# A one-layer trunk on one core: first products of the later MLP blocks run ahead, the second half's norm placed between them, stores issued from GpSimd

## The chip, the core and the metric

The kernel is one program on one NeuronCore of a Trainium2 chip. Its engines are TensorE (PE, with a separate row for weight loads, PEld), VectorE (DVE), ScalarE (ACT), GpSimd (POOL) and SyncE (SP, which here only issues DMA transfers). The metric is the device time of one execution in microseconds (us); lower is better.

## The reference

One layer over 1024 tokens with 1024 features, all in float32. What matters here is the order of the norms and the size of the MLP:

```python
z = rms_norm(h) @ w_in                 # input projection
...                                    # convolution, attention, short convolution, pooling
h = h + rms_norm(mix @ w_out)          # mix: the four mixers side by side
hn = rms_norm(h)
ff = jnp.square(relu(hn @ w_up)) @ w_down       # 1024 -> 4096 -> 1024
h = h + rms_norm(ff)
gate = sigmoid(rms_norm(h) @ w_gate)
h = h + rms_norm((p @ w_proj) * gate)
```

Each rms_norm needs a sum over all 1024 features of a token, so no column of `hn` is known before every block of `mix @ w_out` for that token is done.

## The kernel before

Everything is held transposed: features on the 128 partitions, tokens along a row. The 1024 tokens are two halves of 512 (hf 0 and hf 1). A float32 operand is split in two pieces, hi and lo, one by an ACT cast (L127) and one by a DVE subtraction (L128), and each product of two blocks is three matmuls (hi·hi, hi·lo, lo·hi) of 128x512.

The stages follow one another: input projection and mixers, `out_proj(0)`, `out_proj(1)` (8 blocks of 24 matmuls each, for one half of the tokens), the MLP, and the gate with the output.

The MLP is cut by features in four blocks, c = 0 to 3, each an up group and a down group. A group is one Strassen-Winograd step with seven products, named by p and run in the order 1, 2, 6, 5, 7, 4, 3 (`ORD`). A product is 48 matmuls: four output blocks (mp) of twelve. For an up group the operand on the right is `hn` in quarters: p=1 and p=2 use quarters of the first half of the tokens alone; p=6 and those after it use sums in which both halves stand. So p=1 and p=2 need only `mix_norm(0)`, and the others `mix_norm(1)` too. The right operands of p=1, 2, 6, ... are written to `t_d` in DRAM once, and read back by the later blocks (`Stored`).

`mix_norm(hf)` is the two norms between `out_proj` and the MLP: a sum of squares over blocks, the column sums on PE (L190), a short chain of small DVE operations (L193 to L202), a broadcast on PE (L204) that ACT copies to SBUF (L206), then per block a multiply by it (L806), the residual from `xT` added (L807), the store to `h_d`, a square on ACT (L215) and a sum on DVE (L216); then again L190 to L206, and the scaling L816. The `xT` blocks come through two buffers (`R2`).

Each engine works through its instructions in the written order, apart from small moves of a scheduler; generators in `bg` are advanced by `pump` between products. SP issues every load and nearly every store, in one queue: a store in it waits for the operation that makes its data, and all that stands behind waits too. Before the change SP holds 52 stores of this part (8 `m_d`, 16 `h_d`, 28 `t_d`).

In the old order PE does: `out_proj(1)` with `mix_norm(0)` between its blocks, L190 and L204 of `mix_norm(1)`, p=1 of block 0, p=1 of block 1 (`g1a`, kept in the two `Q` tiles by `Early`), p=2 of block 0, then p=6 of block 0 and the rest. MLP weights come by 1 MB loads (4 for each group) into the six `raw` buffers of 8 KB a partition, which are opened only when the mixers' buffers are closed, after `out_proj(1)`.

What comes ahead of a product is prepared during the product before it: `prep_left` (sums of weight quarters on DVE, 128x2048 each), `prep_right` (right operand), `prep_piece` (hi and lo of one half of the weights).

Of the kernel before, what the change touches and what calls it, by code (L numbers as in the profile page):

```python
# [48 lines left out]
def trunk_layer(ctx, tc, xT, xt, pT, vec, w_in, w_vf, w_pw, w_pool, w_out, w_up, w_down,  # L49
# [6 lines left out]
    psp = ctx.enter_context(tc.tile_pool(name="psp", bufs=1, space=bass.MemoryType.PSUM))  # L56

    BUFS = {"X": 8, "Q": 2, "XS": 6, "F": 8, "U": 2, "W": 4, "TM": 4, "R2": 2, "TC": 5, "TY": 2, "B": 2,
            "P": 2, "V": 4, "PT": 2, "R": 2, "raw": 6, "WG": 10, "G": 1, "GR": 2}
    pools = {}  # L60

    def open_pools(stack, *tags):
        for t in tags:
            pools[t] = stack.enter_context(tc.tile_pool(name=f"p{t}", bufs=1, reuse_waits="tile"))

    open_pools(ctx, "X", "Q", "XS", "F", "U", "W", "TM", "R2", "TC", "TY", "B")
    mixer = ExitStack()
    open_pools(mixer, "P", "V", "PT", "R")
    cnt = [0]

    def uid(s):
# [51 lines left out]
    def store(dst, src, q=nc.sync):  # L123
        q.dma_start(out=dst, in_=src)
# [628 lines left out]
    sq1 = [None, None]  # L753
    mg = [None] * KT

    def out_proj(hf, npump):
        sq1[hf] = tmp("TY")
        for ft in range(KT):
            wh, wl = ws.get(f"o{ft}")
            ps = bank()  # L760
            for i, k in enumerate(YORD):
                spread(i, npump, 10 if hf == 0 else 0)
                mm3(ps, wh[:, k], wl[:, k], y[k][hf][:, 0], y[k][hf][:, 1], i == 0, i == KT - 1)
            with tc.high_priority():
                acc_sq(ps, sq1[hf], ft == 0)
            if hf == 0:
                m = tmp()
            else:
                if ft % 2 == 0:
                    mg2 = slot("F", [P, 2, HALF])  # L770
                m = mg2[:, ft % 2]
                mg[ft] = m
            with tc.high_priority():
                nc.scalar.activation(m, ps, AF.Copy, scale=vcol("g_mix_post", ft))
            if hf == 0:
                store(m_d[ft], m)
# [5 lines left out]
    def split_t(i, k, src):  # L782
        t = slot("X", [P, 2, HALF], F32R)
        split(src, t[:, 0], t[:, 1])
        if i is not None:
            store(t_d[i, k], t.bitcast(F32))
        return t

    t1st = {}
# [1 line left out]
    def mix_norm(hf):  # L791
        bc = rstd_from_sq([sq1[hf]], HALF, 1.0 / D)
        yield
        sq2 = tmp("TY")
        ms = []
        for ft in range(KT):
            if hf == 0:
                if ft % 2 == 0:
                    m2 = slot("U" if ft < 4 else "F", [P, 2, HALF])
                m = m2[:, ft % 2]  # L800
                load(m, m_d[ft])
            else:
                m = mg[ft]
            raw = aux()
            load(raw, xT[ft][:, hs(hf)])
            nc.vector.tensor_mul(m, m, bc)  # L806
            nc.vector.tensor_add(m, m, raw)  # L807
            store(h_d[ft][:, hs(hf)], m)
            acc_sq(m, sq2, ft == 0, "TC")
            ms.append(m)  # L810
            yield
        bc2 = rstd_from_sq([sq2], HALF, 1.0 / D)
        yield
        hq[0, hf], hq[1, hf] = ms[0:4], ms[4:8]
# [6 lines left out]
    load_y(0)
    out_proj(0, 16)
    pump(1000)
    pumpc(1000)
    load_y(1)
    bg.append(mix_norm(0))
    out_proj(1, 3)
    pump(100)
    mixer.close()
    top = ExitStack()  # L830
    open_pools(top, "raw")


    ff = [None] * KT
    sqf = [None, None]

    class Group:

# [2 lines left out]
            self.kind, self.c, self.a = kind, c, {}  # L841

        def load(self, i, j):
            r = self.a[i, j] = slot("raw", [P, 2048])
            if self.kind == "up":
                f = 8 * self.c + 4 * i
                load(r.rearrange("p (m k n) -> p m k n", m=4, k=4),
                     w_up[f:f + 4, :, 4 * j:4 * j + 4].rearrange("m p k n -> p m k n"))
            else:
                load(r.rearrange("p (b k n) -> p b k n", b=2, k=4),  # L850
                     w_down[2 * self.c + j, 2 * i:2 * i + 2].rearrange("b p k n -> p b k n"))

        def combine(self, p):

            a = self.a
            if p == 1:
                return a[0, 0]
            if p == 2:
                return a[0, 1]
            if p == 6:  # L860
                nc.vector.tensor_sub(a[0, 0], a[0, 0], a[1, 0])
                s2 = a["s2"] = slot("raw", [P, 2048])
                nc.vector.tensor_sub(s2, a[1, 1], a[0, 0])
                nc.vector.tensor_add(a[1, 0], a[1, 0], a[1, 1])
# [76 lines left out]
    class Up:  # L941
# [29 lines left out]
        def out(self, p, mp, ps):  # L971
# [23 lines left out]
            else:  # L995
                add(r[0, 1], ps, r[0, 1])
                self.act(r[0, 1])

    class Early:


        def __init__(self):
            q = [slot("Q", [P, 2, HALF]) for _ in range(2)]
            self.p1 = [q[i // 2][:, i % 2] for i in range(4)]

        def start(self, p):
            pass

        def out(self, p, mp, ps):
            nc.scalar.copy(self.p1[mp], ps)  # L1010

    class Down:

# [69 lines left out]
    def product(n, pump_n=0):  # L1083
        p, g, right, outs, banks = seq[n]
        if n + 1 < len(seq):
            prep_left(n + 1)
            prep_right(n + 1)
            prep_piece(n + 1, 0)
        outs.start(p)
        t, s, _ = prepared.pop(n)  # L1090
        key = g, banks or CHAIN[p]
        new = key not in held
        held.setdefault(key, [])
        for mp in range(4):
            if new:
                held[key].append(bank(SETS[key[1]][mp]))
            ps = held[key][mp]
            for k in range(4):
                lh, ll = g.cols(s[mp // 2], mp, k)
                first = new and k == 0  # L1100
                mm(ps, lhsT=lh, rhs=t[k][:, 0], start=first, stop=False, skip_group_check=True)  # L1101
                mm(ps, lhsT=lh, rhs=t[k][:, 1], start=False, stop=False, skip_group_check=True)  # L1102
                end[0] = mm(ps, lhsT=ll, rhs=t[k][:, 0], start=False, stop=(k == 3), skip_group_check=True)  # L1103
            outs.out(p, mp, ps)
            pump(pump_n)
            if mp == 1 and n + 1 < len(seq):
                prep_piece(n + 1, 1)
                loads_after(n + 1)
# [92 lines left out]
    g1a = Group("up", 1)
    ups[0].load(0, 0)
    g1a.load(0, 0)
    ups[0].load(0, 1)
    ups[0].load(1, 0)
    ups[0].load(1, 1)
    early = Early()
    given = Given(t1st)
    first = Up(0)
    seq.append((1, ups[0], given, first, None))  # L1210
    seq.append((1, g1a, given, early, "C"))
    seq.append((2, ups[0], given, first, None))
    right0 = Right(hq, True)
    add_group(ups[0], right0, first, ORD[2:])
    add_group(downs[0], Right(first.r, False), Down(0, False), ORD)
    for c in range(1, 4):
        u = Up(c, early.p1 if c == 1 else None)
        add_group(ups[c], Stored(), u, ORD[1:] if c == 1 else ORD)
        last = c == 3
        add_group(downs[c], Right(u.r, False), Down(c, last), (1, 2, 6, 7, 4, 5, 3) if last else ORD)  # L1220
    prep_left(0)
    prep_right(0)
    for h in range(2):
        prep_piece(0, h)
    for _ in mix_norm(1):
        pass
    for n in range(len(seq)):
        if n == len(seq) - 2:
            bg.append(ff_norm(0))
        product(n, 2 if n >= len(seq) - 2 else 0)  # L1230
# [95 lines left out]
```

## Time and profile before

| | |
|---|---|
| three runs | 1189.30, 1193.99, 1195.81 us; median 1193.99 |
| the profiled execution | 1192.21 us, its span 1190.5 us |
| PE busy | 1142.7 us, 96% of the span |
| DVE busy | 882.8 us, 74% |
| ACT busy | 603.1 us, 51% |
| POOL busy | 15.3 us, 1% |
| mean granted TensorE clock | 0.982 |

The span is what the profile sees of the 1192.21 us; 1.7 us lie outside it. An engine's busy time says how full it is over all stages, and PE's busy time also counts stretches in which its clock was granted at half: such a stretch is busy and yet lasts twice as long. The granted clock is therefore read beside busy time; 1.00 is 2.4 GHz, 0.50 is 1.2 GHz.

### The profile page before, as it was taken

The numbers are of one execution on the slowest core, as the hardware profiler recorded it, in microseconds if no ns is written. First come the engines' busy times: TensorE is split into PE (matmuls) and PEld (weight loads), VectorE is DVE, ScalarE is ACT, GpSimd is POOL, SyncE is SP. The second block draws the span as 40 slices with busy tenths as digits, with TensorE's granted clock in tenths as the row PEclk, the third lists the DMA queues.
The fourth block names the chain that finished last, engine by engine and source line by source line (L and its number), as shares of the span: only waits on it lengthen the run. The fifth ranks groups of instructions, "written<-read, shape, count | busy, mean of one in ns | idle before, by whom it ended". The sixth has DMA issues, their size and how long they took to land.

```text
span 1190.5 us, 14348 instructions
## 1 busy us (share of the span) xinstructions
PE 1142.7 (96%) x5276; PEld 926.1 (78%) x5276; DVE 882.8 (74%) x1419; ACT 603.1 (51%) x1001; POOL 15.3 (1%) x40
## 2 busy tenths in 40 slices
PE   7999999999999969699999999999999999998997
PEld 5788868778878748588888888888888888886876
DVE  6489679986944788859864599734997439999765
ACT  6511474565654445466533654246542455555664
POOL 2100000000000000000000000000000000000000
PEclk9999999999999979899999999999999999999899
DMA  8311121110445775570337503576034760024243
GB/s 319 127 47 54 62 80 37 45 45 27 131 149 190 247 296 181 197 269 29 107 133 258 210 1 107 177 274 220 1 106 134 273 230 1 1 97 150 80 133 124
DMA packets 58885, 159.16 MB, mean 134 GB/s; under 512 B 5952, under 2 KB 6080, under 8 KB 58816
## 3 DMA queue, kind: packets, MB, share of 16 engines
q1 hardware_dynamic: 57536, 154.06, 37.0%
q0 software_dynamic: 1280, 4.20, 0.9%
q8 instruction: 41, 0.67, 0.2%
q14 instruction: 28, 0.23, 0.1%
HBM read 124.68 MB, written 33.55 MB: 133 GB/s over the span
## 4 chain that ended last, share of the span: by engine, by line
PE 82%; DVE 8%; DMA 4%; ACT 3%; issue 2%; SPq 0%; POOL 0%; DVEq 0%; ACTq 0%; POOLq 0%
PE pm L163 7%; PE pm L164 7%; PE pm L165 7%; PE pm L1103 5%; PE pm L1102 5%; PE pS L1103 5%; PE pS L1102 5%; PE pm L1101 5%; PE pS L1101 5%; PE pT L1103 4%; PE pT L1101 4%; PE pT L1102 4%; PE pV L1102 2%; PE pV L1101 2%; PE pV L1103 2%
## 5 line engine op out<-in xcount | busy, mean ns | idle before, releaser
L127 ACT CAST XS<-raw 128x1024 fp32r<-128x1024 f32 x112 | 117.6, 1052 | 154.0 <-PE pm L1102 44.6
L128 DVE TENSOR_TENSOR XS<-raw,XS 128x1024 fp32r<-128x1024 f32 x112 | 136.5, 1220 | 71.5 <-ACT XS L127 71.0
L1101 PE MATMUL pm<-X,XS 128*128 128x512 f32 x248 | 98.5, 398 | 13.3 <-ACT X L127 8.5
L1103 PE MATMUL pm<-X,XS 128*128 128x512 f32 x248 | 97.8, 394 | 2.1 <-DVE XS L128 2.1
L1102 PE MATMUL pm<-X,XS 128*128 128x512 f32 x248 | 98.1, 396 | 0.9 <-DVE X L128 0.9
L1101 PE MATMUL pS<-X,XS 128*128 128x512 f32 x248 | 96.7, 391 | 0.0
L1102 PE MATMUL pS<-X,XS 128*128 128x512 f32 x248 | 96.5, 389 | 0.0
L1103 PE MATMUL pS<-X,XS 128*128 128x512 f32 x248 | 96.5, 389 | 0.0
L1102 PE MATMUL pT<-X,XS 128*128 128x512 f32 x236 | 92.6, 393 | 0.0
L1103 PE MATMUL pT<-X,XS 128*128 128x512 f32 x236 | 91.9, 389 | 0.0
L1101 PE MATMUL pT<-X,XS 128*128 128x512 f32 x236 | 91.8, 389 | 0.0
L380 DVE SCALAR_TENSOR_TENSOR TC<-U,vecs,TC 128x512 f32<-128x512 f32 (+17 forms) x120 | 86.3, 737 | 2.2 <-ACT TC L376 0.8
L163 PE MATMUL pm<-X,W 128*128 128x512 f32 x192 | 79.2, 413 | 0.0
L164 PE MATMUL pm<-X,W 128*128 128x512 f32 x192 | 77.9, 406 | 0.0
L165 PE MATMUL pm<-X,W 128*128 128x512 f32 x192 | 76.9, 400 | 0.0
L128 DVE TENSOR_TENSOR W<-R,W 128x1024 fp32r<-128x1024 f32 (+1 forms) x34 | 41.6, 1222 | 36.2 <-ACT W L127 35.9
L1101 PEld LDWEIGHTS pm<-X,XS 128*128 128x128 f32 x248 | 47.6, 192 | 25.1 <-ACT X L127 9.0
L127 ACT CAST W<-R 128x1024 fp32r<-128x1024 f32 (+1 forms) x34 | 35.7, 1049 | 50.9 <-PE pm L164 45.5
L1103 PEld LDWEIGHTS pm<-X,XS 128*128 128x128 f32 x248 | 47.4, 191 | 12.7 <-DVE XS L128 2.8
L1102 PEld LDWEIGHTS pm<-X,XS 128*128 128x128 f32 x248 | 47.4, 191 | 11.5 <-DVE X L128 1.6
L1101 PEld LDWEIGHTS pS<-X,XS 128*128 128x128 f32 x248 | 46.9, 189 | 9.8
L1103 PEld LDWEIGHTS pS<-X,XS 128*128 128x128 f32 x248 | 46.5, 187 | 9.7
(528 smaller groups left out, 2763.9 us busy)
## 6 DMA issues: line engine op xcount, KB each, us to landing
X<-t_d SPq DMA_DIRECT2D x80, 512.0 KB, 6.0
raw<-in_w_up_dram SPq DMA_DIRECT2D x17, 1024.0 KB, 5.1
raw<-in_w_down_dram SPq DMA_DIRECT2D x16, 1024.0 KB, 5.1
t_d<-X SPq DMA_DIRECT2D x28, 512.0 KB, 3.5
R<-in_w_in_dram SPq DMA_DIRECT2D x16, 512.0 KB, 3.5
R<-in_w_out_dram SPq DMA_DIRECT2D x16, 512.0 KB, 3.6
F<-in_xt_dram SPq DMA_DIRECT2D x8, 512.0 KB, 7.8
proj_d<-TM POOLq DMA_DIRECT2D x16, 256.0 KB, 4.7
```

The costliest lines, as they stand in the source:

```text
L127: copy(hi, raw)
L128: nc.vector.tensor_sub(lo, raw, hi)
L163: mm(ps, lhsT=lh, rhs=rh, start=first, stop=False)
L164: mm(ps, lhsT=lh, rhs=rl, start=False, stop=False)
L165: end[0] = mm(ps, lhsT=ll, rhs=rh, start=False, stop=last)
L380: nc.vector.scalar_tensor_tensor(acc[j][:, lo:], u[j][:, o + lo - s:o + HALF - s], vcol("w_dw", j * TAPS + TAPS - 1 - s), acc[j][:, lo:], ...
L1101: mm(ps, lhsT=lh, rhs=t[k][:, 0], start=first, stop=False, skip_group_check=True)
L1102: mm(ps, lhsT=lh, rhs=t[k][:, 1], start=False, stop=False, skip_group_check=True)
L1103: end[0] = mm(ps, lhsT=ll, rhs=t[k][:, 0], start=False, stop=(k == 3), skip_group_check=True)
```

## The change

The buffers of 8 KB a partition are shared out anew. The pool `P` (two tiles, used by attention) stays open to the end; `raw` has 4 buffers instead of 6, and a ring (`wslot`) hands out P, P, raw, raw, raw, raw. Gate weights, which had ten `WG` tiles, now have six and four halves of P tiles.

The sequence of products starts with p=1 of blocks 1, 2 and 3 (`pre`), then p=1 and p=2 of block 0. Block 1's result is kept in `Q` as before; those of blocks 2 and 3 go through `TM` to DRAM (`p1_d`) and come back into `Q` ahead of their block's p=2. Blocks 2 and 3 then run six products instead of seven, and their p=6, 5 and 4 add the early result on DVE where ACT copied before: 24 additions of 128x512. The number of products in all is unchanged.

`mix_norm(1)` is pumped, two steps behind each block of the first products. The second broadcast of each norm is put behind PE's latest product (`issue_after`), for hf 0 three steps later. The weights of the first two products are loaded into the P tiles ahead of `out_proj(1)`, and split into pieces from its sixth block on, as written; the scheduler places the first pieces at attention's end. The stores to `m_d`, `h_d`, `t_d` and `p1_d` (60 in all) are issued from GpSimd.

```diff
-            "P": 2, "V": 4, "PT": 2, "R": 2, "raw": 6, "WG": 10, "G": 1, "GR": 2}
+            "P": 2, "V": 4, "PT": 2, "R": 2, "raw": 4, "WG": 6, "G": 1, "GR": 2}
...
-                store(m_d[ft], m)
+                store(m_d[ft], m, nc.gpsimd)
...
-            store(t_d[i, k], t.bitcast(F32))
+            store(t_d[i, k], t.bitcast(F32), nc.gpsimd)
...
-            store(h_d[ft][:, hs(hf)], m)
+            store(h_d[ft][:, hs(hf)], m, nc.gpsimd)
...
-        bc2 = rstd_from_sq([sq2], HALF, 1.0 / D)
+        if hf == 0:
+            for _ in range(3):
+                yield
+        with tc.issue_after(end[0].ins):
+            bc2 = rstd_from_sq([sq2], HALF, 1.0 / D)
...
+    def wslot():
+        ring[0] += 1
+        return slot("P" if (ring[0] - 1) % 6 < 2 else "raw", [P, 2048])
...
         def out(self, p, mp, ps):
-            nc.scalar.copy(self.p1[mp], ps)
+            t = self.p1[mp] if self.keep else tmp()
+            nc.scalar.copy(t, ps)
+            if not self.keep:
+                store(p1_d[self.c, mp], t, nc.gpsimd)
...
+    early = [Early(c, c == 1) for c in range(1, 4)]
+    pre = [Group("up", c) for c in range(1, 4)]
+    for c in range(3):
+        seq.append((1, pre[c], given, early[c], "AC"[c % 2 == 0]))
     seq.append((1, ups[0], given, first, None))
-    seq.append((1, g1a, given, early, "C"))
     seq.append((2, ups[0], given, first, None))
...
-        u = Up(c, early.p1 if c == 1 else None)
-        add_group(ups[c], Stored(), u, ORD[1:] if c == 1 else ORD)
+        blk = Up(c, early[c - 1])
+        add_group(ups[c], Stored(), blk, ORD[1:])
...
+    pre[0].load(0, 0)
+    pre[1].load(0, 0)
     load_y(1)
     bg.append(mix_norm(0))
-    out_proj(1, 3)
+    out_proj(1, 3, first_left)
     pump(100)
+    prep_right(0)
     mixer.close()
...
-    for _ in mix_norm(1):
-        pass
+    bg.append(mix_norm(1))
     for n in range(len(seq)):
...
-        product(n, 2 if n >= len(seq) - 2 else 0)
+        if n == npre - 1:
+            pump(100)
+        product(n, 2 if n < npre - 1 or n >= len(seq) - 2 else 0)
```

The order on PE, where `out_proj(1)` ends. Before, its last matmuls (L163 to L165) are followed by the two PE steps of `mix_norm(1)`'s first norm, and then by the first product (L1101 to L1103):

```order
L164 MATMUL pm_4030<-PT_3614,W_3996 128x512
L165 MATMUL pm_4030<-PT_3614,W_3997 128x512
L190 MATMUL pc_4086<-ones,TY_3617 128x1 x4
L204 MATMUL pc_4107<-TC_4102,ones 128x512
L1101 MATMUL pm_4213<-X_3871,XS_4078 128x512
L1102 MATMUL pm_4213<-X_3871,XS_4078 128x512
```

After the change the same place of PE reads as follows (product lines are now L1124 to L1126):

```order
L165 MATMUL pm_4045<-PT_3621,W_3997 128x512
L1124 MATMUL pT_4094<-X_3913,XS_3936 128x512
L1125 MATMUL pT_4094<-X_3913,XS_3936 128x512
...
L1126 MATMUL pT_4094<-X_3972,XS_3937 128x512
L190 MATMUL pc_4108<-ones,TY_3624 128x1 x4
L1124 MATMUL pT_4140<-X_3913,XS_3936 128x512
...
L1125 MATMUL pT_4140<-X_3972,XS_3936 128x512
L204 MATMUL pc_4129<-TC_4124,ones 128x512
L1126 MATMUL pT_4140<-X_3972,XS_3937 128x512
```

L190 now stands behind 12 matmuls of the first product, and L204 behind 11 more. `XS_3936` is a piece of the weights in a P tile; `XS_4078` was one of a `raw` tile.

The second norm of `mix_norm(1)` on PE. Before, its L190 stands in the third product and its L204 two matmuls ahead of the first matmul of p=6 (operand `X_4353`):

```order
L1101 MATMUL pV_4409<-X_3958,XS_4305 128x512
L190 MATMUL pc_4174<-ones,TY_4111 128x1 x4
L1102 MATMUL pV_4409<-X_3958,XS_4305 128x512
...
L204 MATMUL pc_4195<-TC_4190,ones 128x512
L1102 MATMUL pT_4425<-X_3983,XS_4305 128x512
L1103 MATMUL pT_4425<-X_3983,XS_4306 128x512
L1101 MATMUL pm_4213<-X_4353,XS_4369 128x512
```

After, L190 is behind the first matmul of the third product's third block, L204 in the fourth product, and p=6 (operand `X_4501`) follows behind the fifth product:

```order
L1124 MATMUL pV_4387<-X_3913,XS_4305 128x512
L190 MATMUL pc_4262<-ones,TY_4133 128x1 x4
L1125 MATMUL pV_4387<-X_3913,XS_4305 128x512
...
L204 MATMUL pc_4283<-TC_4278,ones 128x512
L1126 MATMUL pS_4457<-X_3913,XS_4384 128x512
...
L1126 MATMUL pV_4557<-X_4033,XS_4454 128x512
L1124 MATMUL pm_4425<-X_4501,XS_4517 128x512
```

Between L204 and the first matmul of p=6 there are now 58 matmuls.

The order on POOL: before, nothing follows its last memset but the end of the program. After, its queue carries all stores of this part, in the order in which their data are made (a piece of it; `p_d` is `p1_d`):

```order
L124 DMA t_d<-X_4033 128x1024
L124 DMA h_d<-F_3700 128x512 x2
L124 DMA p_d<-TM_4251 128x512
L124 DMA h_d<-F_3828 128x512 x2
L124 DMA p_d<-TM_4300 128x512
L124 DMA p_d<-TM_4322 128x512
L124 DMA h_d<-F_3934 128x512
```

Stores that make `p1_d` stand behind stores of `h_d` that wait for `mix_norm(1)`.

## Rows read from the trace of the kernel before

**Rows 1.** The page: busy time of each engine, share of the span, instructions.

```profile
PE 1142.7 (96%) x5276; PEld 926.1 (78%) x5276; DVE 882.8 (74%) x1419; ACT 603.1 (51%) x1001; POOL 15.3 (1%) x40
```

**Rows 2.** Windows: length, busy time (instructions) by engine, PE's granted clock, DMA share, GB/s.

```profile
620.00:700.00 80.00, 80.00 (x355) 66.24 (x354) 50.68 (x58) 38.57 (x56) 0.00 (x0) 1.00 0.51 184
860.00:880.00 20.00, 20.00 (x90) 16.55 (x89) 19.80 (x29) 9.17 (x13) 0.00 (x0) 1.00 0.16 54
```

**Rows 3.** Windows as in rows 2, between 411 and 496 us.

```profile
411.00:417.00 6.00, 4.53 (x17) 3.78 (x18) 3.28 (x13) 0.48 (x2) 0.00 (x0) 0.72 0.36 125
429.00:434.00 5.00, 1.27 (x9) 0.97 (x8) 4.10 (x14) 1.89 (x4) 0.00 (x0) 1.00 1.01 380
434.00:441.00 7.00, 2.04 (x2) 0.50 (x2) 4.15 (x8) 2.66 (x4) 0.00 (x0) 0.51 1.01 358
441.00:448.00 7.00, 4.75 (x11) 3.34 (x12) 6.11 (x8) 1.99 (x3) 0.00 (x0) 0.52 1.04 387
...
481.00:489.00 8.00, 0.00 (x0) 0.00 (x0) 8.00 (x13) 2.40 (x4) 0.00 (x0) 0.77 0.00 0
489.00:496.00 7.00, 5.79 (x14) 4.11 (x15) 7.00 (x13) 4.17 (x8) 0.00 (x0) 0.53 0.43 171
```

**Rows 4.** Waits of PE, whole span: us in all, times, longest.

```profile
PE pc L190 <- DVE TY L216: 3.2, 2, 1.7
```

**Rows 5.** Timeline behind `out_proj(1)`: start, us, engine, operation, [idle before, releaser].

```profile
428.82 0.40 PE L165 MATMUL pm<-PT,W 128*128 128x512 f32 x1
...
430.75 1.05 PE L190 MATMUL pc<-ones,TY 128*128 128x1 f32 x8 [1.53 <-DVE TY L216]
...
432.11 5.42 SPq L121 DMA_DIRECT2D raw<-in_w_up_dram  x5
...
434.30 2.04 PE L204 MATMUL pc<-TC,ones 128*128 128x512 f32 x2 [2.50 <-DVE TC L202]
...
437.00 1.29 DVE L806 TENSOR_TENSOR F<-F,B 128x512 f32<-128x512 f32 x2 [2.85 <-ACT B L206]
...
441.15 0.80 PE L1101 MATMUL pm<-X,XS 128*128 128x512 f32 x1 [4.80 <-ACT XS L127]
```

**Rows 6.** Timeline of `mix_norm(1)` on DVE, and around the first p=6.

```profile
459.00 1.29 DVE L807 TENSOR_TENSOR F<-F,R 128x512 f32<-128x512 f32 x2
...
464.88 1.28 DVE L807 TENSOR_TENSOR F<-F,R 128x512 f32<-128x512 f32 x2
...
470.63 1.28 DVE L807 TENSOR_TENSOR F<-F,R 128x512 f32<-128x512 f32 x2
...
473.96 1.05 PE L190 MATMUL pc<-ones,TY 128*128 128x1 f32 x8
...
479.23 1.10 PE L204 MATMUL pc<-TC,ones 128*128 128x512 f32 x2
...
481.43 5.38 DVE L816 SCALAR_TENSOR_TENSOR F<-F,vecs,B 128x512 f32<-128x512 f32 x8
...
489.32 1.22 PE L1101 MATMUL pm<-X,XS 128*128 128x512 f32 x2 [8.54 <-ACT X L127]
```

**Rows 7.** DMA issues of 400 to 520 us: count, size, median us to landing.

```profile
t_d<-X SPq DMA_DIRECT2D x24, 512.0 KB, 3.6
raw<-in_w_up_dram SPq DMA_DIRECT2D x5, 1024.0 KB, 10.1
...
R<-in_xT_dram SPq DMA_DIRECT2D x10, 256.0 KB, 3.8
```

**Rows 8.** DMA issues of POOL, whole span: count, size, median us to landing.

```profile
proj_d<-TM POOLq DMA_DIRECT2D x16, 256.0 KB, 4.7
```

**Rows 9.** POOL's groups: busy us, mean ns of one issue, idle before by releaser.

```profile
L124 POOL DMA_DIRECT2D proj_d<-TM x16 | 9.0, 565 | 30.7 <-DVE TM L292 20.8 <-ACT TM L294 6.2 <-DVE rs_v L279 1.4
```

**Rows 10.** Timeline of ACT at attention's end.

```profile
328.33 0.62 ACT L127 CAST Q<-R 128x512 fp32r<-128x512 f32 x1
...
333.49 0.62 ACT L127 CAST V<-R 128x512 fp32r<-128x512 f32 x1 [2.70 <-DMA R<-y_d]
```

More of the change, by code (lines that the diff above doesn't have):

```diff
@@ L64, in open_pools @@
             pools[t] = stack.enter_context(tc.tile_pool(name=f"p{t}", bufs=1, reuse_waits="tile"))
-    open_pools(ctx, "X", "Q", "XS", "F", "U", "W", "TM", "R2", "TC", "TY", "B")
+    open_pools(ctx, "X", "Q", "XS", "F", "U", "W", "TM", "R2", "TC", "TY", "B", "P")
     mixer = ExitStack()
-    open_pools(mixer, "P", "V", "PT", "R")
+    open_pools(mixer, "V", "PT", "R")
     cnt = [0]
@@ L754, in trunk_layer, with out_proj @@
     mg = [None] * KT
-    def out_proj(hf, npump):
+    def out_proj(hf, npump, hook=None):
         sq1[hf] = tmp("TY")
         for ft in range(KT):
+            if hook and ft == 5:
+                hook()
             wh, wl = ws.get(f"o{ft}")
@@ L819, in mix_norm @@
             yield
[L821 to L826, printed above, removed]
-    out_proj(1, 3)
[L828 to L831, printed above, removed]
     ff = [None] * KT
     sqf = [None, None]
+    ring = [0]
+    def wslot():
+        ring[0] += 1
+        return slot("P" if (ring[0] - 1) % 6 < 2 else "raw", [P, 2048])
     class Group:
@@ L843, in load @@
         def load(self, i, j):
-            r = self.a[i, j] = slot("raw", [P, 2048])
+            r = self.a[i, j] = wslot()
             if self.kind == "up":
@@ L861, in combine @@
                 nc.vector.tensor_sub(a[0, 0], a[0, 0], a[1, 0])
-                s2 = a["s2"] = slot("raw", [P, 2048])
+                s2 = a["s2"] = wslot()
                 nc.vector.tensor_sub(s2, a[1, 1], a[0, 0])
@@ L997, in out, with __init__, alloc, fetch @@
                 self.act(r[0, 1])
+    p1_d = tc.dram_tile([4, 4, P, HALF], F32, name="p1_d")
     class Early:
-        def __init__(self):
+        def __init__(self, c, keep):
+            self.c, self.keep, self.p1 = c, keep, None
+            if keep:
+                self.alloc()
+        def alloc(self):
             q = [slot("Q", [P, 2, HALF]) for _ in range(2)]
             self.p1 = [q[i // 2][:, i % 2] for i in range(4)]
+        def fetch(self):
+            if self.p1 is None:
+                self.alloc()
+                for mp in range(4):
+                    load(self.p1[mp], p1_d[self.c, mp])
+        def __getitem__(self, mp):
+            return self.p1[mp]
         def start(self, p):
@@ L1088, in product @@
             prep_piece(n + 1, 0)
+            nxt = seq[n + 1]
+            if nxt[0] == 2 and getattr(nxt[3], "early", None) is not None:
+                nxt[3].early.fetch()
         outs.start(p)
@@ L1137, in gate_rstd @@
             bc3[hf] = rstd_cols([sq3[hf]], HALF, 1.0 / D, "rs_g", "pm")
-    GT = ["WG"] * 8, ["WG"] * 2 + ["XS"] * 6
+    GT = ["WG"] * 6 + ["P"] * 2, ["P"] * 2 + ["XS"] * 6
     wg = [[None] * KT, [None] * KT]
@@ L1147, in gate_w @@
                 load(raw, w_gate[k][:, hs(cf)])
-                t = slot(GT[cf][k], [P, 2, HALF], F32R)
+                if GT[cf][k] != "P":
+                    t = slot(GT[cf][k], [P, 2, HALF], F32R)
+                elif k % 2 == 0:
+                    t2 = slot("P", [P, 2, 2, HALF], F32R)
+                    t = t2[:, 0]
+                else:
+                    t = t2[:, 1]
                 split(raw, t[:, 0], t[:, 1])
@@ L1198, in finish, with first_left @@
             nc.sync.dma_start(out=out[tb][:, hs(cf)], in_=e)
[L1201 to L1207, printed above, removed]
+    early = [Early(c, c == 1) for c in range(1, 4)]
+    pre = [Group("up", c) for c in range(1, 4)]
     given = Given(t1st)
     first = Up(0)
+    for c in range(3):
+        seq.append((1, pre[c], given, early[c], "AC"[c % 2 == 0]))
     seq.append((1, ups[0], given, first, None))
-    seq.append((1, g1a, given, early, "C"))
     seq.append((2, ups[0], given, first, None))
-    right0 = Right(hq, True)
-    add_group(ups[0], right0, first, ORD[2:])
+    npre = len(seq)
+    add_group(ups[0], Right(hq, True), first, ORD[2:])
     add_group(downs[0], Right(first.r, False), Down(0, False), ORD)
     for c in range(1, 4):
-        u = Up(c, early.p1 if c == 1 else None)
-        add_group(ups[c], Stored(), u, ORD[1:] if c == 1 else ORD)
+        blk = Up(c, early[c - 1])
+        add_group(ups[c], Stored(), blk, ORD[1:])
         last = c == 3
-        add_group(downs[c], Right(u.r, False), Down(c, last), (1, 2, 6, 7, 4, 5, 3) if last else ORD)
-    prep_left(0)
-    prep_right(0)
-    for h in range(2):
-        prep_piece(0, h)
-    for _ in mix_norm(1):
-        pass
+        add_group(downs[c], Right(blk.r, False), Down(c, last), (1, 2, 6, 7, 4, 5, 3) if last else ORD)
+    load_y(0)
+    out_proj(0, 16)
+    pump(1000)
+    pumpc(1000)
+    pre[0].load(0, 0)
+    pre[1].load(0, 0)
+    load_y(1)
+    bg.append(mix_norm(0))
+    def first_left():
+        prep_left(0)
+        for h in range(2):
+            prep_piece(0, h)
+    out_proj(1, 3, first_left)
+    pump(100)
+    prep_right(0)
+    mixer.close()
+    top = ExitStack()
+    open_pools(top, "raw")
+    pre[2].load(0, 0)
+    for i in range(2):
+        for j in range(2):
+            ups[0].load(i, j)
+    bg.append(mix_norm(1))
     for n in range(len(seq)):
@@ L1229, in trunk_layer @@
             bg.append(ff_norm(0))
[L1230 removed]
+        if n == npre - 1:
+            pump(100)
+        product(n, 2 if n < npre - 1 or n >= len(seq) - 2 else 0)
     pump(100)
```

## The prediction

> **What bounds the kernel now.** The table of busy times comes first: PE is busy 96% of the span [rows 1]. Over most of the MLP it also runs at full rate: from 620 to 700 us it is never idle, its granted clock is 1.00, and 355 matmuls take 80 us, so 0.2254 us each and 48 x 0.2254 = 10.8 us for a product. DVE has slack in such an up group (50.7 of 80 us) and little in the stretch 860 to 880, where it is busy for 19.8 of 20 us [rows 2]. So this change can win or lose only where PE stands still or runs at half clock.
>
> The windows between 411 and 496 show where that is [rows 3]. From 429 to 448, 19 us, PE has 22 records, and the timeline tells what they are: eight of L190, two of L204 and some twelve product matmuls [rows 5]. At full clock L190 takes 1.05 us and L204 1.10 [rows 6], so the 19 us hold 1.05 + 1.10 + 12 x 0.2254 = 4.9 us of work: **14.1 us lost**. Part of that is clock: after the idle of 429 to 441 the granted clock is 0.52 from 441 to 448, almost all at 1.2 GHz instead of 2.4. From 481 to 496, 15 us, there are 14 matmuls, 3.2 us of work: **11.8 lost**, again idle first (8.54 us) and then 0.53 of the clock [rows 3, 6]. From 411 to 417 PE idles 6.00 - 4.53 = 1.5 us and the clock averages 0.72, which takes another 0.28 x 6 = 1.7: **3.2 lost**. Its wait is L190 for the sum of squares of `mix_norm(0)`; the two such waits are 3.2 us together, the longest 1.7 [rows 4].
>
> The timeline gives the reasons. `out_proj(1)` ends at 428.82 + 0.40 = 429.2; I call this moment T0. L190 waits for its last sum, the first norm's broadcast follows, and the weights of the first product are issued by SP only at 432.11, so that the first product starts at 441.15, held by the ACT cast of a weight piece [rows 5]. The second gap is a chain on DVE: p=6 needs the second norm, whose scaling L816 starts 2.20 us behind L204 and whose first usable operand comes 489.32 - 481.43 = 7.9 us after that [rows 6]. Nothing independent was left for PE at either place.
>
> **The change, part by part.** *First products ahead, weights in P.* Product 0 needs the first half's operands and weights that now lie in SBUF since attention's end. It can start at T0, and the chain of the first norm lies beside it. PE reaches L190 after 12 matmuls (T0 + 2.7) and L204 after 1.05 us more and 11 matmuls: T0 + 6.2. From L190 to L204 the old chain took 434.30 - 430.75 = 3.55, so the same T0 + 6.25: no wait. The 14.1 us should go whole. If the cover were gone (the pieces or the first half's operands not ready), the price is again up to 14.1.
>
> *The second half's norm between them.* L204 now takes 1.1, and L806 came 437.00 - (434.30 + 2.04) = 0.66 behind it [rows 5]: T0 + 8.0, up to T0 + 9 since a weight subtraction stands ahead of it on DVE. After 1.29 us of multiplications the first pair of residual additions (L807) can run, T0 + 9.3 to 10.3; its two `xT` loads are there. The six further loads go through two buffers, so three rounds follow. In the old trace the pairs start at 459.00, 464.88 and 470.63, 5.8 us apart, and L190 follows the last by 473.96 - 470.63 = 3.3 [rows 6]. So L190 can run at T0 + 9.3 + 17.4 + 3.3 = T0 + 30.0, or 31.0. PE comes to it after 121 product matmuls and the first norm's two steps: 27.3 + 1.05 + 1.10 = T0 + 29.4. **A wait of 1.1 us stays** (0.6 to 1.6), and I add the 1.7 us that the clock cost after the 1.7 us wait at 411: **2.8**. The bounds are 0 (rounds a little shorter) and, with loads late, those of the first rival.
>
> From there PE runs 49 matmuls to L204: T0 + 30.5 + 1.05 + 1.7 + 11.0 = T0 + 44.3. DVE has 13.8 us for the chain that took 479.23 - 473.96 = 5.3 before. L816 starts at T0 + 46.5, the first operand of p=6 is there at T0 + 54.4 and all four some 3 us later. PE comes to p=6 after 228 product matmuls: 51.4 + 4.3 for both norms + 2.8 = T0 + 58.5. The cover is 1 to 4 us. Bounds 0 and 1, **taken as 0.3**; beyond the cover every late us is a lost one.
>
> *The norm of the first half.* Its L190 stands behind one matmul of `out_proj(1)`'s sixth block, where it stood behind fifteen, but its loads no longer stand behind stores in SP. Bounds 0 and the old 3.2; **1.0**, nearer to 0, as the sums ahead of it are fewer.
>
> *Weights at attention's end.* Two casts of 128x1024 come into ACT's queue there, at most two 128x512 casts each, 4 x 0.62 = 2.5 us, and ACT idles 2.70 us before 333.49 [rows 10]. Hidden, if the load has landed; if not, the casts of attention behind them wait. Between 0 and 1.5: **0.7**.
>
> *The rest.* The 24 additions are 24 x 0.64 = 15.4 us of DVE (L807, two in 1.28), in up groups where DVE has 29 of 80 us free: 0; without that cover 15.4. ACT gives up as many copies. Eight fetches and two more weight loads (2 MB) on SP lie under groups of 65 us: 0. The 60 stores on POOL cost 60 x 0.565 = 34 us [rows 9] of an engine busy for 15.3; what waits for them is told with the third rival. The tail keeps its work; its gate weights find other buffers, and I bound that by 2 us either way and take 0.
>
> **Sum.** Lost before 14.1 + 11.8 + 3.2 = 29.1; after 2.8 + 0.3 + 1.0 + 0.7 = 4.8. The profiled execution of 1192.2 would become 1167.9. The median of the runs is 1.8 us above it: **1169.5**. A difference below 0.5% (6 us) is more than this measurement can tell from none.
>
> **The rivals.** *1. The `xT` loads land late.* Four 1 MB weight loads are issued at about T0, ahead of the second pair of `xT` loads. Weight loads took 10.1 us to land there, `xT` loads 3.8 [rows 7]. One round at 10.1 adds 6.3 us of wait at L190, 1176; all three add 18.9, 1188.5, hardly a change. For it: DMA moved 358 to 387 GB/s from 434 to 448 while such loads ran [rows 3]. Against it: four loads are 4.2 MB, at that rate 11 us, so that only the first round meets them. The page "DMA: Bandwidth & Descriptors" of the Trainium skill (Issuing engines are not separate DMA queues) says that transfers of all issuing engines share the same 16 DMA engines, so stores moved to POOL make no room; that would favour this rival, and the shares near 1.0 from 429 to 448 fit it.
>
> *2. The additions fall where DVE is full.* If the shortened blocks push them into stretches like 860 to 880, they cost up to 15.4: 1185. Against it: block 1 already ran with six products and such additions, and PE was never idle between 620 and 700 [rows 2].
>
> *3. Slower: late stores.* Operand tiles of the up group of block 0 are used again two products later, and the new contents may not be written until the store to `t_d` has landed. Four issues of 0.565 and a landing of 4.7 [rows 8, 9] make 7.0 us, where about 20 of the 21.6 us of two products are free. It begins to cost from a landing of 17.7 us, and at 22.6 the five products p=6 to p=3 lose 4.9 each, all of the gain; at 24 us they lose 31, and the kernel takes 1201. Against it: the old POOL stores landed in 4.7. The page "SBUF — State Buffer" of the Trainium skill (Who interferes with whom) says that a DMA of GpSimd must wait for its descriptors while certain DVE operations (copy, cast, tensor_scalar in a two-port mode) hold a shared port, whereas operations with two inputs only block GpSimd's reads. By it the busy DVE would delay these stores little, since those groups are almost all two-input operations; no run yet shows it.
>
> *4. The first weights land late* at attention's end: at 10.1 us the casts hold ACT for some 5 us, and with the clock that loses 6.5: 1176.
>
> **Chances.** Likeliest 0.58 (its own range 1164 to 1175); better than it, with no wait left, 0.05; rival 1 with one round 0.15, with three 0.05; rival 2, 0.06; rival 4, 0.05; rival 3, 0.06. Faster by over 0.5% are all but rival 1 with three rounds (same) and rival 3 (slower): 0.89, 0.05, 0.06. The range 1161 to 1182 holds the likeliest, half of the better one, and the cases at 1176, with the 3 us that runs differ from their median: about 0.8.
>
> **What would show it.** Right: product 0 starts within 1 us of the last matmul of `out_proj(1)`; PE's idle time between there and the second product after p=6 is below 5 us, with at most one stretch of half clock; p=6 starts without a wait; PE stays at 20.00 of 20 us in the up groups of blocks 2 and 3. Wrong: L190 of the second norm waits over 4 us for the last sum, or DVE waits for `xT` loads; PE idles at attention's end; DVE waits for POOL's stores ahead of operand subtractions; additions of early results release PE late.

## The result, and the profile after

The changed kernel takes 1180.4 us (median; 1179.6 to 1182.1) beside 1193.1 for the kernel before on the same chips: a ratio of 0.9899, interval 0.9874 to 0.9923. That is 12.7 us, inside the forecast range of 1161 to 1182, but only about half of the 24.3 that the sum gave. The profiled execution has a span of 1178.9 us, 11.6 less than before.

The windows of the changed kernel, as in [rows 2, 3], show PE at 20 of 20 us everywhere from 520 to 1040 and two places where it still stands still:

```profile
407.00:410.00 3.00, 0.54 (x3) 0.11 (x2) 1.98 (x3) 1.50 (x3) 0.54 (x1) 1.00 0.91 303
410.00:416.00 6.00, 6.00 (x24) 4.92 (x25) 3.53 (x12) 1.35 (x4) 0.00 (x0) 0.72 0.22 75
...
459.00:469.40 10.40, 0.24 (x2) 0.00 (x0) 4.58 (x6) 3.88 (x6) 2.32 (x5) 0.70 0.71 266
469.40:475.00 5.60, 5.53 (x17) 4.76 (x18) 3.65 (x6) 0.90 (x3) 0.54 (x1) 0.50 0.23 90
475.00:480.00 5.00, 5.00 (x19) 3.96 (x19) 2.39 (x3) 1.42 (x2) 0.54 (x1) 0.81 0.14 52
```

From 459 to 469.4 PE is idle for 10.40 - 0.24 = 10.16 us and then runs at half clock: 0.50 x 5.6 + 0.19 x 5.0 = 3.75 us more, 13.9 in all. At 407 to 416 it is 2.5 us of idle time and 0.28 x 6 = 1.7 of clock. The timeline of PE names the instruction in both places:

```profile
409.91 1.05 PE L190 MATMUL pc<-ones,TY 128*128 128x1 f32 x8 [2.46 <-DVE TY L216]
...
429.51 0.40 PE L165 MATMUL pm<-PT,W 128*128 128x512 f32 x1
429.74 0.39 PE L1124 MATMUL pT<-X,XS 128*128 128x512 f32 x1
432.46 0.95 PE L190 MATMUL pc<-ones,TY 128*128 128x1 f32 x8
...
435.92 1.10 PE L204 MATMUL pc<-TC,ones 128*128 128x512 f32 x2
...
469.47 1.86 PE L190 MATMUL pc<-ones,TY 128*128 128x1 f32 x8 [10.23 <-DVE TY L216]
...
500.70 0.50 PE L1126 MATMUL pm<-X,XS 128*128 128x512 f32 x1 [0.26 <-DVE XS L128]
```

The first product follows the last matmul of `out_proj(1)` without a gap (before: 441.15, 12 us behind it [rows 5]), the steps of the first norm wait for nothing, and p=6 waits 0.26 us where it waited 8.54 [rows 6]. What is left is L190, once for each half of the tokens, waiting for a sum of squares. DVE and SP show why the second sum is late. The residual additions (L809, L807 of [rows 6]) wait for their `xT` blocks:

```profile
439.70 1.28 DVE L809 TENSOR_TENSOR F<-F,R 128x512 f32<-128x512 f32 x2
...
451.37 0.69 DVE L809 TENSOR_TENSOR F<-F,R 128x512 f32<-128x512 f32 x1 [5.04 <-DMA R<-in_xT_dram]
...
455.03 0.69 DVE L809 TENSOR_TENSOR F<-F,R 128x512 f32<-128x512 f32 x1 [0.67 <-DMA R<-in_xT_dram]
...
460.35 0.69 DVE L809 TENSOR_TENSOR F<-F,R 128x512 f32<-128x512 f32 x1 [2.03 <-DMA R<-in_xT_dram]
...
467.27 0.69 DVE L809 TENSOR_TENSOR F<-F,R 128x512 f32<-128x512 f32 x1 [2.84 <-DMA R<-in_xT_dram]
```

and SP had issued four 1 MB weight loads ahead of them, and one more ahead of the last:

```profile
428.54 3.39 SPq L121 DMA_DIRECT2D raw<-in_w_up_dram  x4
440.41 15.67 SPq L121 DMA_DIRECT2D R<-in_xT_dram  x5
456.89 0.38 SPq L121 DMA_DIRECT2D raw<-in_w_down_dram  x1
458.34 0.33 SPq L121 DMA_DIRECT2D R<-in_xT_dram  x1
```

The first of the later `xT` loads, issued at 440.41, is used at 451.37; the last, issued at 458.34, at 467.27. The DMA issues of 425 to 480 us, to be read beside [rows 7]:

```profile
raw<-in_w_up_dram SPq DMA_DIRECT2D x4, 1024.0 KB, 16.3
t_d<-X POOLq DMA_DIRECT2D x6, 512.0 KB, 7.2
h_d<-F POOLq DMA_DIRECT2D x8, 256.0 KB, 5.1
p_d<-TM POOLq DMA_DIRECT2D x7, 256.0 KB, 4.7
R<-in_xT_dram SPq DMA_DIRECT2D x6, 256.0 KB, 6.8
```

The median of the `xT` loads hides their spread. The two that SP issued first, behind the four weight loads, took 11.0 us (issues of 440.0 to 441.3):

```profile
R<-in_xT_dram SPq DMA_DIRECT2D x2, 256.0 KB, 11.0
```

The kernel before had the same late round: the first pair of additions, then the two `xT` loads of 440.0 to 442.0, behind its five weight loads:

```profile
438.21 1.29 DVE L807 TENSOR_TENSOR F<-F,R 128x512 f32<-128x512 f32 x2
R<-in_xT_dram SPq DMA_DIRECT2D x2, 256.0 KB, 10.3
```

There the median of ten, 3.8 [rows 7], hid it, and DVE came to those blocks only at 459.00 [rows 6], when they had long landed.

### The profile page after: what moved, and what is told of

Same layout as the page of the kernel before. It is cut to its first block, busy times and chain, and to the rows that moved or that the text cites. A ratio compares the mean times of both kernels' runs of the same rounds, so it can differ in the third digit from the quotient of the medians.

```text
span 1178.9 us, 14412 instructions
## 1 busy us (share of the span) xinstructions
PE 1139.7 (97%) x5276; PEld 927.3 (79%) x5276; DVE 898.0 (76%) x1443; ACT 593.5 (50%) x985; POOL 47.6 (4%) x100
## 4 chain that ended last, share of the span: by engine, by line
PE 81%; DVE 7%; DMA 6%; ACT 3%; issue 2%; SPq 0%; POOL 0%; DVEq 0%; ACTq 0%; POOLq 0%
PE pm L163 7%; PE pm L164 7%; PE pm L165 7%; PE pm L1126 4%; PE pS L1125 4%; PE pS L1126 4%; PE pS L1124 4%; PE pm L1125 4%; PE pm L1124 4%; PE pT L1124 4%; PE pT L1125 4%; PE pT L1126 4%; DMA R<-in_xT_dram 3%; PE pV L1125 2%; PE pV L1126 2%
## 5 line engine op out<-in xcount | busy, mean ns | idle before, releaser
L127 ACT CAST XS<-raw 128x1024 fp32r<-128x1024 f32 x76 | 79.9, 1051 | 108.5 <-PE pT L1125 35.9
L128 DVE TENSOR_TENSOR XS<-raw,XS 128x1024 fp32r<-128x1024 f32 x76 | 92.7, 1220 | 19.3 <-ACT XS L127 19.0
L1125 PE MATMUL pT<-X,XS 128*128 128x512 f32 x248 | 97.1, 392 | 0.0
L1124 PE MATMUL pT<-X,XS 128*128 128x512 f32 x248 | 96.9, 391 | 0.0
L1126 PE MATMUL pT<-X,XS 128*128 128x512 f32 x248 | 96.9, 391 | 0.0
L1126 PE MATMUL pS<-X,XS 128*128 128x512 f32 x240 | 93.8, 391 | 0.0
L1126 PE MATMUL pm<-X,XS 128*128 128x512 f32 x240 | 93.3, 390 | 0.3 <-DVE XS L128 0.3
L1125 PE MATMUL pm<-X,XS 128*128 128x512 f32 x240 | 93.4, 389 | 0.0
L1124 PE MATMUL pm<-X,XS 128*128 128x512 f32 x240 | 93.4, 389 | 0.0
L1125 PE MATMUL pS<-X,XS 128*128 128x512 f32 x240 | 93.4, 389 | 0.0
L1124 PE MATMUL pS<-X,XS 128*128 128x512 f32 x240 | 93.4, 389 | 0.0
L163 PE MATMUL pm<-X,W 128*128 128x512 f32 x192 | 79.5, 414 | 0.0
L165 PE MATMUL pm<-X,W 128*128 128x512 f32 x192 | 76.5, 399 | 0.0
L127 ACT CAST XS<-P 128x1024 fp32r<-128x1024 f32 x36 | 37.8, 1051 | 59.9 <-PE pT L1125 18.1
L128 DVE TENSOR_TENSOR W<-R,W 128x1024 fp32r<-128x1024 f32 (+1 forms) x34 | 41.5, 1222 | 30.3 <-ACT W L127 30.2
L1126 PEld LDWEIGHTS pT<-X,XS 128*128 128x128 f32 x248 | 46.6, 188 | 10.2 <-issue 0.5
L1124 PEld LDWEIGHTS pT<-X,XS 128*128 128x128 f32 x248 | 46.7, 189 | 9.8
L1125 PEld LDWEIGHTS pT<-X,XS 128*128 128x128 f32 x248 | 46.7, 188 | 9.8 <-issue 0.2
L1126 PEld LDWEIGHTS pm<-X,XS 128*128 128x128 f32 x240 | 45.0, 187 | 10.3 <-DVE XS L128 1.0
```

Source lines behind the costliest of these rows:

```text
L127: copy(hi, raw)
L128: nc.vector.tensor_sub(lo, raw, hi)
L163: mm(ps, lhsT=lh, rhs=rh, start=first, stop=False)
L165: end[0] = mm(ps, lhsT=ll, rhs=rh, start=False, stop=last)
```

## The experiments

Theory A: the second norm's sum is late since its `xT` loads stand behind the weight loads. Rival B: the stores on GpSimd crowd or delay the transfers. All times are medians, and ratios are to the kernel before on the same chip. That took 1192.8 us beside e1 to e4, 1191.0 beside e5 to e8 and 1193.3 beside e9 to e12; between these sets, and with the change, the ratios compare better than the times. T0 is where the first product starts when it follows `out_proj(1)` directly. Except where said, the kernels differ from the change by their diff alone, but the scheduler may then place PE's steps anew, and that turned out to matter.

**Stores back on SP (e1).** `store(..., nc.gpsimd)` becomes `store(...)` in all four places.

> All 60 stores issued from SP again, everything else as in the change. Theory A (the xT loads of the second half's norm come late because they stand in SP's queue and on the DMA engines behind four 1 MB weight loads): they now also stand behind h_d and p1_d stores that wait for their data, so L190 of that norm waits 12 to 20 us instead of 10.2, and the kernel takes 1183 to 1190. Rival B (GpSimd's 60 stores crowd the DMA engines or are issued late, and that is what delays the xT loads): L190 waits less than 7 us and the kernel takes 1177 or less.

1170.7 us (ratio 0.9820, 0.9795 to 0.9844): faster than the change, so the expectation of theory A failed, and by time alone rival B looked right. PE's timeline says otherwise:

```profile
467.11 1.05 PE L190 MATMUL pc<-ones,TY 128*128 128x1 f32 x8 [0.17 <-DVE TY L216]
486.62 0.74 PE L1124 MATMUL pm<-X,XS 128*128 128x512 f32 x2 [2.18 <-ACT X L127]
```

T0 is 425.6, so L190 comes at T0 + 41.5 and has just waited for its sum: the sum is no earlier than in the change (T0 + 39.7). It is late for the cause that theory A gave, `xT` loads held in SP's queue by three `p1_d` stores:

```profile
437.28 1.49 SPq L121 DMA_DIRECT2D R<-in_xT_dram  x2
...
442.03 5.76 SPq L124 DMA_DIRECT2D p_d<-TM  x3
...
448.36 0.41 SPq L121 DMA_DIRECT2D R<-in_xT_dram  x1
```

What had moved is the place of the two L190 on PE, 14 and 52 matmuls later: PE had other work ahead of them. With the order not held, the time of this run can't tell what the queue is worth. Its landings tell something, those of the weight loads and of the first two late `xT` loads:

```profile
raw<-in_w_up_dram SPq DMA_DIRECT2D x4, 1024.0 KB, 9.8
R<-in_xT_dram SPq DMA_DIRECT2D x2, 256.0 KB, 8.7
```

The weight loads land in 9.8 us, not 16.3, but, counted from T0, are issued 4 us later, behind the `t_d` stores; the first late `xT` load lands at T0 + 20.6, where it did at T0 + 21.5 in the change.

**The second half's `xT` blocks first (e2).** Into the two R2 buffers and three W tiles that `out_proj` has left:

```diff
+    for ft in range(KT):
+        if ft < 2:
+            xr.append(aux())
+        else:
+            if ft % 2 == 0:
+                w2 = slot("W", [P, 2, HALF])
+            xr.append(w2[:, ft % 2])
+        load(xr[ft], xT[ft][:, hs(1)])
     pre[2].load(0, 0)
```

> The eight xT blocks of the second half are loaded before the weight loads, two into the R2 buffers and six into the W buffers that out_proj has just left. Theory A: all eight land by about T0 + 8, L190's wait falls from 10.2 us to under 1.5, DVE never waits for xT; a wait of 1 to 3 us at L204 may come up, as it stands 11 rows behind L190 in this order; 1169 to 1173. Rival B, or a norm that is bound by DVE's own work: L190 still waits 5 us or more, 1176 or more.

1164.9 us (0.9773, 0.9750 to 0.9796). DVE never waits for `xT`, and PE runs through:

```profile
454.08 1.05 PE L190 MATMUL pc<-ones,TY 128*128 128x1 f32 x8 [0.40 <-DVE TY L216]
...
457.63 1.10 PE L204 MATMUL pc<-TC,ones 128*128 128x512 f32 x2
```

T0 is 426.9, so the sum is there at T0 + 27.2, 12.5 us earlier than in the change; L204 doesn't wait. The time is below the expected 1169 to 1173, partly since T0 itself is 2.8 us earlier in this profile.

**The weights behind the `xT` loads (e3).** The two buffers stay; block 0's first load goes behind the fourth `xT` load, the others behind the eighth:

```diff
-            load(raw, xT[ft][:, hs(hf)])
+            xl = nc.sync.dma_start(out=raw, in_=xT[ft][:, hs(hf)])
+            if hf == 1 and ft in LATE:
+                with tc.issue_after(xl.ins):
+                    for ij in LATE[ft]:
+                        ups[0].load(*ij)
```

> Block 0's four weight loads are issued behind xT loads: the first behind the fourth, the other three behind the eighth; the two xT buffers stay. Theory A: xT loads land in 3 to 5 us, the rounds are 5 to 6 us as before the change, L190 waits 0 to 4 us, 1171 to 1175. Rival B (stores of GpSimd crowd the engines): landings stay at 6 us or more and the time within 2 us of the change, 1178 to 1182. Should the late weights hold products 3 to 5, PE shows a wait for a weight piece instead.

1175.6 us (0.9860, 0.9841 to 0.9879).

```profile
460.62 0.59 PE L190 MATMUL pc<-ones,TY 128*128 128x1 f32 x2 [6.09 <-DVE TY L216]
```

T0 is 429.3, so the sum is there at T0 + 31.3. That is what the prediction's rounds through two buffers gave (T0 + 30.0 to 31.0). L190 waits 6.1, not 0 to 4, since in this order PE reaches it 4 us earlier. So block 0's weight loads ahead cost 39.7 - 31.3 = 8.4 us of the sum's time, and the two buffers, with one weight load still between the rounds, another 31.3 - 27.2 = 4.1.

**Only the two L190 later (e4).**

```diff
-        if hf == 0:
-            for _ in range(3):
-                yield
+        for _ in range(7 if hf == 0 else 17):
+            yield
```

> Only the places of two PE steps: L190 of the first half's norm behind 15 matmuls of the sixth block instead of one, L190 of the second half's behind 168 product matmuls instead of 121. Nothing about the loads. If the sums are late by as much as PE's waits say (2.5 and 10.2 us) and p=6 has cover left, both waits go, with the half clock behind each: p=6 then waits 1 to 3 us, 1166 to 1171. If the chain behind L190 (small DVE steps, L204, scaling, first operands) has no cover left, the wait moves to p=6: 1174 to 1178.

1171.6 us (0.9829, 0.9801 to 0.9857), at the upper end of what was expected. Neither L190 waits, but p=6 loses cover: L204 of the second norm waits 3.4 us, p=6 1.8, and at one place PE waits 1.7 for ACT's copy of an early result to `TM`:

```profile
458.35 0.50 PE L1123 MATMUL pT<-X,XS 128*128 128x512 f32 x1 [1.74 <-ACT TM L1027]
```

**Only the first L190 later (e9)**, the 7 of the last diff alone.

> Of the change, only L190 of the first half's norm is moved, behind 15 matmuls of the sixth block. T0 falls from 429.7 by 4 to 5.5 us. The weight loads wait for out_proj(1) to free their buffers, so if the late xT loads hang on them, L190 of the second norm keeps its distance of about T0 + 39.7 and the kernel takes 1174.5 to 1177. If that L190 keeps its moment (about 469 us) instead, the gain is given back there: 1179 to 1181.

1175.2 us (0.9851, 0.9836 to 0.9866). T0 falls to 425.4, and L190 of the second norm comes at 465.03, T0 + 39.7 as in the change, after a wait of 10.15. The late loads hang on T0, as the weight loads ahead of them do. The first norm's wait of 2.5 us, 4.2 with its half clock, is worth 5.2 us by the medians; T0 fell by 4.4.

**The `xT` blocks first and the first L190 later**, with the stores on GpSimd (e5) and then on SP (e6). L190 and L204 stand at the same places on PE in both; elsewhere the scheduler has moved a dozen matmuls.

> e2 (xT blocks into the W buffers, ahead of the weights) with L190 of the first half's norm behind 15 matmuls of the sixth block. If the two losses are apart, T0 falls from 426.9 to about 424.6 and the MLP keeps e2's length: no wait above 1.5 us from 400 to 520, 1160 to 1163. If they are not, the first half's operands come too late for the first product and PE waits there: 1164 or more.

> e5 with all 60 stores on SP; the order on PE is the same, so the stores' queue alone differs. Theory A (a store matters only where a load stands behind it, and no xT load does here): within 3 us of e5, 1159 to 1165. Rival B (GpSimd's stores are themselves slow and cost time): 2 us or more below e5. Rival D (SP's queue holds loads of later blocks behind stores): over 4 us above e5.

1162.9 (0.9768, 0.9751 to 0.9784) and 1162.4 us (0.9756, 0.9733 to 0.9779): no difference. But they don't lose at the same place. With the stores on GpSimd it is the second norm's L190 that waits, with the stores on SP the first norm's:

```profile
451.73 1.05 PE L190 MATMUL pc<-ones,TY 128*128 128x1 f32 x8 [1.10 <-DVE TY L216]
409.73 1.05 PE L190 MATMUL pc<-ones,TY 128*128 128x1 f32 x8 [1.12 <-DVE TY L216]
```

Windows from 424 to 520 us of the first:

```profile
424.00:520.00 96.00, 94.90 (x416) 77.36 (x415) 78.74 (x118) 55.56 (x90) 20.02 (x38) 0.98 0.66 254
```

and of the second:

```profile
424.00:520.00 96.00, 95.90 (x426) 78.20 (x425) 81.16 (x122) 57.12 (x92) 0.00 (x0) 1.00 0.69 261
```

(the change: 85.51 us busy at a clock of 0.93). The second has the better window; T0 is 426.3 there, 2.4 us later than in the first, and both profiles span 1161.0 us. So rival B has fallen as far as time goes: with L190 and L204 held on PE and the `xT` loads first, the queue moves a wait from one norm to the other and is worth nothing in sum, which is in part luck. What it is worth by itself where the `xT` loads stand behind the weights, as in the change, no run shows.

**Only block 1's first product ahead**, in the change (e7) and then with the `xT` blocks first (e11).

```diff
-    for c in range(3):
-        seq.append((1, pre[c], given, early[c], "AC"[c % 2 == 0]))
+    seq.append((1, pre[0], given, early[0], "C"))
...
-        add_group(ups[c], Stored(), blk, ORD[1:])
+        add_group(ups[c], Stored(), blk, ORD[1:] if c == 1 else ORD)
```

> Of the change without the first products of blocks 2 and 3 ahead: only block 1's runs ahead, blocks 2 and 3 run seven products, nothing goes through p1_d. If the two products are the cover of p=6, the second norm's sum comes as late as before (T0 + 39 to 41), L190 waits 10 to 13 us, and p=6 waits another 6 to 11 us where it waited 0.3: 1188 to 1195. If p=6 had cover to spare, 1180 to 1184.

> e2 with only block 1's first product ahead, as in e7. p=6 then comes 21.7 us earlier on PE, at about T0 + 37, and its operands at T0 + 45 to 48: a wait of 8 to 11 us with half clock behind it, 1174 to 1179. If two products less of cover still hide the chain: 1163 to 1167.

1185.8 (0.9959, 0.9940 to 0.9979) and 1182.2 us (0.9905, 0.9890 to 0.9920): the first better than the 1188 to 1195 expected, since L190 waits 5.6 us and not 10 to 13, the second a little worse than expected. In both p=6 waits long; of the first:

```profile
485.60 1.22 PE L1124 MATMUL pm<-X,XS 128*128 128x512 f32 x2 [11.27 <-ACT X L127]
```

The two further products are p=6's cover. By the ratios they are worth 0.6%, some 7 us, in the change, where L190 takes most of it back, and 1.3%, some 16, where it doesn't (by the medians 5.4 and 17.3).

**The first weights in `raw` buffers**, in the change (e8) and then with the `xT` blocks first (e10).

```diff
-    ring = [0]
+    ring = [2]
...
-    pre[0].load(0, 0)
-    pre[1].load(0, 0)
...
-    pre[2].load(0, 0)
+    for g in pre:
+        g.load(0, 0)
+    first_left()
+    prep_right(0)
```

> Of the change without the weights in P: the ring starts with the raw buffers, so the first products' weights are loaded when attention's buffers are closed, and the two PE steps of the first norm stand ahead of the first product again. The first product starts 10 to 13 us behind the end of out_proj(1) as in the kernel before: 1189 to 1195. If these weights in P had only moved a wait, 1180 to 1184.

> e2 with the first products' weights in raw buffers, as in e8. e8 cost nothing beside the change, since L190 of the second norm came at the same moment. If that is the reason, the cost shows here, where the sum no longer binds: the first product starts 8 us late with half a clock behind it, and the kernel takes 1173 to 1178, 8 to 13 above e2. If early weights are worth nothing anyway: 1163 to 1167.

1180.3 us (0.9912, 0.9891 to 0.9933), the same as the change: the expectation failed, and its "only moved a wait" came true. The first product starts 8.1 us later than in the change, and L190 waits half as long, at almost the same moment:

```profile
437.88 0.79 PE L1124 MATMUL pT<-X,XS 128*128 128x512 f32 x1
...
466.87 1.86 PE L190 MATMUL pc<-ones,TY 128*128 128x1 f32 x8 [5.04 <-DVE TY L216]
```

With the `xT` blocks first the same edit takes 1180.2 us (0.9891, 0.9876 to 0.9905), some 14 above e2 by the ratios. The first product then waits 6.9 us and starts at 444.01, also because the weights now stand behind six `xT` loads; the 8 to 13 that were expected left that out.

**The second L190 later (e12)**, e5 with 12 more steps ahead of it.

> e5 with L190 of the second norm behind some 130 product matmuls instead of 109, and its L204 40 rows behind it. The 1.1 us that L190 still waits and the half clock go, if p=6 keeps its cover: 1160 to 1162, L190, L204 and p=6 without a wait above 0.3 us. If p=6 loses its cover it waits instead: 1163 or more.

1166.7 us (0.9778, 0.9762 to 0.9794), not the 1160 to 1162 expected; the ratio's interval overlaps that of e5, so that the two can't be told apart. L190 no longer waits, and p=6 does:

```profile
482.61 0.73 PE L1128 MATMUL pm<-X,XS 128*128 128x512 f32 x2 [0.23 <-DVE X L128]
483.60 0.49 PE L1127 MATMUL pS<-X,XS 128*128 128x512 f32 x1 [0.26 <-ACT XS L127]
485.55 0.50 PE L1129 MATMUL pm<-X,XS 128*128 128x512 f32 x1 [1.45 <-DVE XS L128]
```

These 1.9 us stand for e5's 1.1 at L190 and the half clock behind it. From T0 to the last product's start both profiles need 617.8 us: the edit has traded one wait for another. The 4 us by which the profiles differ lie elsewhere: T0 is 2.4 us later (426.27, 423.86), with the same order on PE up to there, and 1.7 lie behind the last product. Their cause is not known.

## Why the prediction was right and wrong

**Where PE lost time, and that the rest would not move: right.** From 520 to 1040 us PE is never idle before or after. The 24 additions and the fetches cost nothing there, and from the last product to the end of the span are 119.8 us, 119.1 before.

**First products at T0: right in place, wrong in worth.** The first product follows directly, and L190 and L204 of the first norm stand at T0 + 2.7 and T0 + 6.2, as worked out. But "the 14.1 us should go whole" does not hold for the end: with the weights in `raw` the same 1180.3 us are reached. The time was taken back 40 us further on, where PE waits for a sum whose moment the early start doesn't change.

**The second norm's chain: the step that failed.** The prediction took the old rhythm of `xT` loads, 5.8 us a round, and got L190 at T0 + 30.0 to 31.0 and 2.8 us lost. L190 came at T0 + 39.7 and lost 13.9. The rhythm came near with most weights behind (T0 + 31.3); but the first round took 11.7 us and the last load 8.9. The first round could have been read from the trace before, whose own late loads took 10.3 us: the prediction spaced its rounds by the last three pairs of additions and left out the one at 438.21, 20.8 us ahead of them. That is rival 1, named with one late round (1176) or three (1188.5). Its argument "only the first round meets them" missed the next weight load, which SP issued ahead of the last `xT` load. And its 11 us for the four loads left out the stores beside them: six of 512 KB to `t_d`, issued from 425.8 to 431.4, make 7.3 MB with the loads, some 20 us (an estimate) at the 360 GB/s measured:

```profile
425.00:450.00 25.00, 25.00 (x113) 20.23 (x112) 17.56 (x34) 11.15 (x19) 4.83 (x9) 1.00 0.99 360
```

The weight loads took 16.3 us to land, not the old 10.1, and the first late `xT` load landed at T0 + 21.5. That the stores lengthen this wait is worked out, not tried by itself; e1, with the same bytes in another queue, has that landing within 1 us. The rule of the page "DMA: Bandwidth & Descriptors" of the Trainium skill (Issuing engines are not separate DMA queues), that stores on GpSimd run on the same engines, agrees with the equal times of e5 and e6. The prediction's own signs of being wrong, L190 waiting over 4 us and DVE waiting for `xT` loads, both came; that the time still fell inside the range is due to its upper end, set by rivals at 1176, and not to the likeliest case (1164 to 1175).

**The first norm: mis-sized.** Taken as 1.0, it lost 2.5 of wait and 1.7 of clock, 4.2. Its sum came earlier than before (409.9, 412.5), as the freed loads suggested, but L190 had been placed 14 matmuls, 3.2 us, earlier still.

**p=6: right** (0.3 forecast, 0.26 measured), and for the reason given: e7 shows 11.3 without the two products. That the sizes agree is luck: the 0.26 us are a wait for the weights' low piece, which DVE splits right behind p=6's operands. **Attention's end:** 0.7 forecast; PE reached the next L190 0.35 us earlier than before (334.86, 335.21), so nothing was lost there.

**Late stores (rival 3): did not happen.** DVE waited for no store; `t_d` landed in a median of 5.4 us over the run, 12.2 at the longest, short of the 17.7 at which it would have cost. By the page "SBUF — State Buffer" of the Trainium skill (Who interferes with whom) a two-input DVE operation is in the way of GpSimd's reads, not of its writes; medians of 4.3 to 5.4 us for the stores to `m_d`, `h_d`, `t_d` and `p1_d`, DVE busy, beside 4.7 for the old POOL stores, do not speak against it. What part of a landing is a wait for descriptors no run shows.

**The sum.** Lost after: 13.9 + 4.2 + 0.3 - 0.35 = 18.0 against 4.8 forecast; 29.1 - 18.0 = 11.1 against the 11.6 by which the span fell.

Of all kernels tried, the four with the `xT` blocks first, the first weights early and three first products ahead (e2, e5, e6, e12) are the fastest: 1162.4 to 1166.7 us, ratios of 0.9756 to 0.9778, some 26 to 29 us below the kernel before. Their intervals overlap, so the later first L190 is not shown to add to e2.

## What to carry to other kernels

When PE is given work to run ahead, find the next instruction that PE must wait for and follow its chain down to the loads: if its moment stays, the early start comes back as a longer wait there. Small loads that a norm needs belong ahead of large ones that are not needed yet, and here it paid more to find them buffers that lay idle at that time (e2, 0.9773) than to move the instruction that waits (e4, 0.9829). A median of landings can hide the one load on which the chain hangs: read that load. When an edit changes a queue, hold PE's order fixed or compare it, for the scheduler may move the waiting instruction, and the time then shows that move and not the queue. Equal times can hide waits that have changed places, as in e5 and e6.

## What the hardware showed that was not expected

Transfers of all queues together came to about 400 GB/s (404 in e5 from 424 to 450 us), and a 1 MB load in that crowd took 16.3 us to land, or 18.0 in e5, where it had no effect on PE. While such loads were in flight, small transfers landed sooner in the queue that did not hold them: in the change the two `h_d` stores of 440.0 to 441.3 on GpSimd took 6.3 us, the two `xT` loads of the same size behind the weights on SP 11.0, and the first four `h_d` stores took 6.2 us on GpSimd (e5) and 10.2 on SP (e6):

```profile
h_d<-F POOLq DMA_DIRECT2D x2, 256.0 KB, 6.3
h_d<-F POOLq DMA_DIRECT2D x4, 256.0 KB, 6.2
h_d<-F SPq DMA_DIRECT2D x4, 256.0 KB, 10.2
```

After an idle stretch of 10.2 us the granted clock was 0.50 for 5.6 us and on average 0.81 for the next 5; after one of 2.5 us it averaged 0.72 over 6. So a wait of 2.5 us and one of 1.7 [rows 3, 4] cost the same in clock.
